# One rotary product for two heads' queries, with the swapped halves moved into the stored key

## The chip, the cores and the metric

The kernel runs on all 8 cores of one Trainium2 chip. Cores 0 to 3 are one die, 4 to 7 the other. Each core works on its own 1024 of the 8192 tokens and the cores do not exchange data. The metric is the device time of the slowest core, in microseconds. A run is "fast" when neither die's granted TensorE clock fell below the other's and its time is within 1.5% of the fastest; in "slow" runs one die runs at a granted clock of 0.81 to 0.98 and the time is up to 18% longer.

## The reference

The operation is a decoder block: a gated convolution and latent attention in parallel, then a gated feed-forward. The part that matters is the query and the key of the attention. There are 16 heads; a query has 128 plain and 64 rotary dimensions, and the 64 rotary dimensions of the key are the same for all heads.

```python
q = (rmsnorm(q_lat, q_a_g) @ w_q_b).reshape(b, s, 16, 192)
# ... k_nope, v from the latent; k_rope shared by all heads
q = apply_rope_tail(rmsnorm(q, q_norm_g), cos, sin)
k = apply_rope_tail(rmsnorm(k, k_norm_g), cos, sin)
y_mla = causal_block_attention(q, k, v) @ w_mla_out

def apply_rope_tail(x, cos, sin):          # on the last 64 of 192
    x1, x2 = split(x_r, 2)                 # 32 and 32
    rot = concat([x1 * cos - x2 * sin, x2 * cos + x1 * sin])
```

## The kernel before

Data lie with features on the 128 partitions (rows) and tokens on the free dimension (columns). One head's query is made in three tiles of 348, 348 and 344 tokens. The rotation needs `x2` where `x1` is, so the weights of each head hold its rotary columns twice, the second time with the halves exchanged; the product gives both copies in one 128-row result, of which only 64 rows are new information.

```python
def QN(t):                                   # plain part, 6 matmuls
    for k in range(6):
        mm(PS[p][:, 0:n], w[:, k, 0:128], qn[:, k, off:off + n], ...)
    act(sqn[:, 0:n], PS[p][:, 0:n], AF.Square, ...)
    act(qraw[:, 0:n], PS[p][:, 0:n], AF.Copy, ...)

def QR(t):                                   # rotary part, 6 matmuls, rows 64..127 are the swapped copy
    for k in range(6):
        mm(PS[p][:, 0:n], w[:, k, 128:256], qn[:, k, off:off + n], ...)
    act(sqr[0:64, 0:n], PS[p][0:64, 0:n], AF.Square, ...)
    tt(qt1[0:64, 0:n], PS[p][0:64, 0:n], CSq[0:64, off:off + n], ALU.mult, ...)
    tt(qt2[0:64, 0:n], PS[p][64:128, 0:n], CSq[64:128, off:off + n], ALU.mult, ...)
    tt(qr_[0:64, 0:n], qt1[0:64, 0:n], qt2[0:64, 0:n], ALU.add, ...)

def QS(t):                                   # sum of squares over rows: 2 matmuls against ones
    mm(PS[p][:, 0:n], ones, sqn[:, 0:n], True, False, ...)
    mm(PS[p][:, 0:n], ones, sqr[:, 0:n], False, True, ...)     # rows 64..127 are zeros
    rsq(rsqh[:, 0:n], PS[p][:, 0:n], 192.0, ...)
    stt(Qn[hb][...], qraw, gqe, rsqh, ALU.mult, ALU.mult, ...)
    tt(Qr[hb][0:64, ...], qr_[0:64], rsqh[0:64], ALU.mult, ...)
```

The score of a block of 128 keys takes two matmuls per query stretch: one with the plain key, one with the rotary key `krope`, whose rows 64 to 127 are zeros (so are those of `Qr`).

The order of instructions is decided when the program is built. Streams of small units (score steps, probability-times-value steps, key, value, query and convolution units) are merged by a list scheduler in the kernel: it keeps an estimate of when each engine is free and takes next the unit that TensorE would wait least for, and among equals the one with the lowest target position `pos`.

```python
t = S.ready(PE, u.need() if callable(u.need) else u.need, u.room) if u.pe else 0.0
...
key = (int(max(0.0, t - S.free[PE]) / 0.1), u.pos)
if best is None or key < best[0]:
    best = (key, s, b)
...
weight = [(912 - A_(kb // 4)) / 960.0 + 0.45 for kb in range(32)]     # where a score step belongs in its head
for us, span in ((kq, 0.85), (vq, 0.95), (qq, 0.85)):                 # next head's units, spread over this head
    for i, u in enumerate(us):
        u.pos = h - 1 + span * i / len(us)
...
rate = (sum(u.pe for u in st_c.units) - 22.0) / (NH + 0.3)            # convolution units per head
```

The constants 0.45, 0.85 and 22.0 are set by hand.

## Time and profile before

| | |
|---|---|
| time, median of 4 fast runs | 2668.1 us |
| attention stage (from the first 390-column matmul to the last attention matmul) | 992.6 us |
| stage before / after it, core 1 | 207.9 / 1465.3 us |

The cores view of before gives each core's span and mean granted clock. This profile fell into a slow run; cores 4 to 7 are left aside.

```profile
core 1: 2665.7 us, clock 0.996
...
core 3: 2662.7 us, clock 0.997
...
core 6: 2922.4 us, clock 0.898
...
die 0 (median of its cores): 2665.0 us, clock 0.997
die 1 (median of its cores): 2914.3 us, clock 0.892
```

The busy line of the page of core 1 (time, share of the span and number of instructions for each engine; PEld is the weight load, which overlaps) and the chain that ended last:

```profile
PE 2578.4 (97%) x18530; PEld 1637.9 (61%) x18530; DVE 1530.1 (57%) x3086; ACT 983.6 (37%) x1716; POOL 192.4 (7%) x330
...
PE 89%; DVE 3%; DMA 3%; issue 2%; ACT 2%; SPq 0%; DVEq 0%; ACTq 0%; POOL 0%; POOLq 0%
```

TensorE is busy 97% of the span, and the chain is 89% TensorE: it is the bound. The stage of interest is attention. The windows view of core 1 over this stage (stretch, its length, then busy time of TensorE, weight loads, VectorE, ScalarE and POOL, the clock, and the DMA share and rate):

```profile
207.00:1201.00 994.00, 969.44 (x7943) 608.13 (x7944) 732.20 (x1825) 688.06 (x1268) 32.72 (x62) 1.00 0.20 39
```

VectorE and ScalarE are busy 74% and 69% of the stage, TensorE 98%. The lines named in the profile are those of helpers: L509 issues the matmuls, L516 the ScalarE operations, L527, L523 and L540 VectorE's operations on two tensors, on two tensors and a scalar, and its copies. (All are one higher after the change.) What TensorE waits for in the stage, from the waits view of core 1 (total us, times, longest):

```profile
PE ps L509 <- ACT arena L516: 9.6, 26, 0.9
PE ps L509 <- DVE arena L527: 7.7, 19, 1.1
PE ps L509 <- DVE arena L523: 3.8, 6, 1.2
PE ps L509 <- DVE arena L540: 0.4, 2, 0.2
```

These are waits of up to 1.2 us, 21.5 us in all, none of which stands out. The matmuls, VectorE and ScalarE operations of the query work, from the groups by shape of core 1 (count, busy us, mean ns of one):

```profile
L509 PE MATMUL ps<-arena 128*128 128x348 bf16 x448 | 81.4, 311 | 2.0 <-ACT arena L516 1.7
...
L509 PE MATMUL ps<-arena 128*128 128x344 bf16 x224 | 40.3, 309 | 0.0
...
L527 DVE TENSOR_TENSOR arena<-ps,arena 64x348 f32<-64x348 f32 x64 | 33.1, 517 | 18.2 <-ACT arena L516 15.3 <-PE ps L509 2.0
...
L527 DVE TENSOR_TENSOR arena<-arena 64x348 f32<-64x348 f32 x32 | 16.2, 508 | 0.9 <-DVE arena L527 0.2
L527 DVE TENSOR_TENSOR arena<-arena 64x348 bf16<-64x348 f32 x32 | 16.2, 506 | 0.0
...
L516 ACT ACTIVATE arena<-ps 64x348 bf16<-64x348 f32 x32 | 14.4, 451 | 16.9 <-PE ps L509 16.8
```

672 matmuls of 348 or 344 columns are the query work. Their mean of 311 ns is not what one costs: matmuls overlap, and their ends are modelled. What one costs is the time from its start to the next one's start, in a run of equal ones: 147 ns for 348 columns.

"Columns" is what the stage's matmuls would take back to back, (columns / 2.4 GHz + 2.5 ns, at least 25 ns) each; this fits the median start to start of every shape that appears in runs within 1.2 ns. "Waits" is the rest: the time from start to start above that. (The waits view shows less: it counts a gap only from the modelled end of a matmul, which for 348 columns lies 311 ns after its start, not 147.)

### The profile page before, as it was taken

The page shows a single profiled execution, that of the slowest core. Times are in us where ns is not written, and L with a number is a line of the kernel's source. Part 1 is how long each engine was busy: PE and PEld are TensorE (multiplying, and loading weights), DVE is VectorE, ACT ScalarE, POOL GpSimd, SP SyncE. Part 2 cuts the span into 40 slices and gives each one's busy share as a digit, 9 for nine tenths or more (in the row PEclk, how much of TensorE's full clock was granted, in tenths as well). Part 3 has the DMA queues.
Part 4 walks back from the last instruction along what each step waited for, and adds up shares of the span by engine and source line. Part 5 has one row for each costly group of instructions (what it writes and reads, how often), then busy time and mean ns, then how long its engine had stood idle before and what let it go on. Part 6 is the DMA issues. An engine that isn't in the chain of part 4 may idle for free.

```text
span 2922.4 us, 51158 instructions; the slowest of 8 cores (2662.7 to 2922.4 us)
## 1 busy us (share of the span) xinstructions
PE 2841.3 (97%) x18415; PEld 1726.9 (59%) x18530; DVE 1534.9 (53%) x3086; ACT 983.2 (34%) x1716; POOL 191.8 (7%) x330
## 2 busy tenths in 40 slices
PE   4999999999999999999999999999999999999999
PEld 2886565656666665666666665554466456645653
DVE  3973777777877777411111112664266436634652
ACT  4864777776777777211101132000000000000000
POOL 1010000000000000000000000000000000000000
PEclk9999999999999999999888888888888888888888
DMA  9663111111202113444334733333433343344346
GB/s 198 153 112 59 22 32 30 36 29 25 44 22 39 20 34 100 80 74 71 59 61 66 173 64 59 64 60 56 73 59 63 56 70 65 54 62 72 59 68 148
DMA packets 65685, 196.68 MB, mean 67 GB/s; under 512 B 7328, under 2 KB 8608, under 8 KB 64416
## 3 DMA queue, kind: packets, MB, share of 16 engines
q0 software_dynamic: 46800, 145.91, 30.8%
q1 hardware_dynamic: 18640, 47.51, 5.0%
q8 instruction: 154, 2.52, 0.3%
q14 instruction: 91, 0.75, 0.1%
HBM read 323.44 MB, written 15.83 MB: 116 GB/s over the span
## 4 chain that ended last, share of the span: by engine, by line
PE 89%; DVE 4%; issue 3%; ACT 2%; DMA 2%; SPq 0%; DVEq 0%; ACTq 0%; POOL 0%; POOLq 0%
PE ps L509 89%; DVE arena L527 2%; ACT arena L516 2%; DVE arena L523 2%; DMA arena<-wkvin 1%; DMA arena<-xg 0%; SPq L543 0%; DVE arena L540 0%; DVEq L196 0%; ACTq L196 0%; DVE arena L533 0%; POOL arena L543 0%; POOLq L196 0%; SPq L196 0%
## 5 line engine op out<-in xcount | busy, mean ns | idle before, releaser
L509 PE MATMUL ps<-arena 128*128 128x390 bf16 (+11 forms) x18415 | 2841.3, 319 | 77.7 <-ACT arena L516 31.8
L509 PEld LDWEIGHTS ps<-arena 128*128 128x128 bf16 x18530 | 1726.9, 102 | 1191.5 <-issue 368.0
L527 DVE TENSOR_TENSOR arena<-ps,arena 128x390 f32<-128x390 f32 (+6 forms) x744 | 378.2, 511 | 1079.4 <-PE ps L509 979.6
L527 DVE TENSOR_TENSOR arena<-arena 128x130 bf16<-128x130 bf16 (+18 forms) x1522 | 669.7, 479 | 249.1 <-ACT arena L516 223.2
L516 ACT ACTIVATE arena<-arena 128x256 f32<-128x256 f32 (+13 forms) x412 | 267.5, 674 | 1114.7 <-DVE arena L523 966.9
L516 ACT ACTIVATE arena<-ps,arena 128x128 bf16<-128x128 f32 (+10 forms) x672 | 440.7, 672 | 499.1 <-PE ps L509 464.3
L523 DVE SCALAR_TENSOR_TENSOR arena<-arena 128x1024 f32<-128x1024 f32 (+9 forms) x499 | 371.9, 762 | 31.6 <-ACT arena L516 5.8
L516 ACT ACTIVATE arena<-ps 128x512 bf16<-128x512 f32 (+13 forms) x627 | 312.8, 515 | 204.8 <-PE ps L509 198.9
L543 POOL DMA_DIRECT2D arena<-wall x294 | 171.5, 584 | 2563.2 <-PE ps L509 2511.7
L536 DVE TENSOR_SCALAR arena<-arena 128x1024 f32<-128x1024 f32 (+1 forms) x90 | 72.3, 804 | 0.0
L523 DVE SCALAR_TENSOR_TENSOR arena<-ps,arena 128x256 bf16<-128x256 f32 (+1 forms) x80 | 33.2, 465 | 12.0 <-PE ps L509 6.9
L540 DVE COPY arena<-ps 128x456 f32<-128x456 f32 (+2 forms) x64 | 27.2, 425 | 2.1 <-PE ps L509 1.1
L543 POOL DMA_DIRECT2D arena<-xg x30 | 16.0, 549 | 141.5 <-PE ps L509 50.6
L533 DVE TENSOR_SCALAR arena<-arena 128x390 f32<-128x390 f32 (+2 forms) x29 | 16.2, 560 | 2.0 <-DVE arena L540 0.2
L516 ACT ACT_TABLE_LOAD x5 | 6.4, 1283 | 30.0 <-DVE arena L523 17.2
L527 DVE TENSOR_TENSOR arena<-arena,ps 128x390 bf16<-128x390 f32 (+1 forms) x24 | 12.3, 511 | 1.3 <-PE ps L509 0.7
L540 DVE CAST arena<-arena 128x1028 f32<-128x1028 int32 (+1 forms) x5 | 3.6, 719 | 4.7 <-DMA arena<-posg 4.3
L540 DVE COPY arena<-arena 128x6 f32<-128x6 f32 (+1 forms) x24 | 3.8, 158 | 1.0
L961 POOL MEMSET arena<- 128x4096 bf16 x1 | 3.6, 3560 | 0.0
L1145 DVE MEMSET arena<- 64x1040 bf16 x2 | 1.9, 925 | 0.4 <-issue 0.4
L767 DVE MEMSET arena<- 128x128 bf16 x1 | 0.2, 165 | 1.2 <-PEq L420 1.2
L543 POOL DMA_DIRECT2D arena<-cst x1 | 0.7, 720 | 0.0
(6 smaller groups left out, 1.2 us busy)
## 6 DMA issues: line engine op xcount, KB each, us to landing
arena<-wall POOLq DMA_DIRECT2D x182, 512.0 KB, 5.3
arena<-wall POOLq DMA_DIRECT2D x64, 352.0 KB, 4.5
arena<-xg POOLq DMA_DIRECT2D x22, 512.0 KB, 9.8
arena<-xo SPq DMA_DIRECT2D x16, 520.0 KB, 20.3
arena<-xg SPq DMA_DIRECT2D x8, 1024.0 KB, 6.3
arena<-wall POOLq DMA_DIRECT2D x32, 256.0 KB, 4.0
outT<-arena SPq DMA_DIRECT2D x32, 256.0 KB, 3.8
arena<-wall POOLq DMA_DIRECT2D x16, 384.0 KB, 4.7
```

Of the source, the lines that this page charges most:

```text
L509: S.add(PE, lambda e: e.matmul(out, lhsT=lhsT, rhs=rhs, start=start, stop=stop), reads, writes, cost=max(width(rhs) / 2400.0, 0.055) + 0.003)
L516: S.add(ACT, lambda e: e.activation(out=out, in_=in_, func=func, **kw), reads, writes, cost=c)
L523: S.add(DVE, lambda e: e.scalar_tensor_tensor(out=out, in0=in0, scalar=scalar, in1=in1, op0=op0, op1=op1), reads, writes, cost=dcost(out, ...
L527: S.add(DVE, lambda e: e.tensor_tensor(out=out, in0=in0, in1=in1, op=op), reads, writes, cost=dcost(out, in0, in1) + held)
L533: S.add(DVE, lambda e: e.tensor_scalar(out=out, in0=in0, scalar1=s1, scalar2=None, op0=op0), reads, writes, cost=c)
L536: S.add(DVE, lambda e: e.tensor_scalar(out=out, in0=in0, scalar1=s1, scalar2=s2, op0=op0, op1=op1), reads, writes, cost=c)
L540: S.add(DVE, lambda e: e.tensor_copy(out=out, in_=in_), reads, writes, cost=dcost(out, in_))
L543: S.add(eng, lambda e: e.dma_start(out=out, in_=in_), reads=reads, writes=writes, chan=chan, cost=in_.shape[0] * width(in_) * esz(in_.dtyp ...
L767: S.add(DVE, lambda e: e.memset(ones, 1.0), writes=[Tones], cost=0.2)
L961: f_h.units.append(Unit(lambda: S.add(POOL, lambda e: e.memset(krope, 0.0), writes=Tkr, cost=3.5), 0.0, pos=-8.0, ok=lambda: not f_w.units ...
L1145: S.add(DVE, lambda e, i_=i_: e.memset(Qr[i_][64:128, :], 0.0), writes=[TQr[i_]])
```

## The change

A score is a sum over rows, so the swap can be done on either side of it. The change stores the key's rotary rows a second time, halves exchanged, in the rows of `krope` that held zeros; the query needs `x * cos` in its first 64 rows and `x * (sin, -sin)` in the others, from the same unswapped `x`. The 64 rows of weight columns that this frees take the next head's rotary columns: one product per pair of heads. The rotary squares are added into the plain ones, so that one matmul against ones is enough.

```diff
 def weight_plan():
-        plan.append((("hq", h), "wq", 0, 6, 256 * h, 256))
+        if h % 2 == 0:
+            plan.append((("hq", h // 2), "wq", 0, 6, 192 * h, 384))
...
-    f_h.units.append(Unit(lambda: S.add(POOL, lambda e: e.memset(krope, 0.0), ...
+    def krot():
+        for r, q in ((64, 32), (96, 0)):
+            dma(SP, krope[r:r + 32, :], krope[q:q + 32, :], "krs%d" % q, reads=Tkr, writes=Tkr)
...
+    def QR(t):                       # in every second head only
+        for k in range(6):
+            mm(PS[p][:, 0:n], w[:, k, 256:384], qn[:, k, off:off + n], k == 0, k == 5, ...)
+        act(sqr[:, t, 0:n], PS[p][:, 0:n], AF.Square, ...)
+        for x, y in ((0, 3), (1, t)):
+            r = slice(64 * x, 64 * x + 64)
+            for o in (slice(0, 64), slice(64, 128)):
+                tt(qrot[o, y, 0:n], PS[p][r, 0:n], CSq[o, off:off + n], ALU.mult, ...)
     def QN(t):
...
+        tt(sqn[r, 0:n], sqn[r, 0:n], sqr[r, t, 0:n], ALU.add, ...)
     def QS(t):
-        mm(PS[p][:, 0:n], ones, sqn[:, 0:n], True, False, ...)
-        mm(PS[p][:, 0:n], ones, sqr[:, 0:n], False, True, ...)
+        mm(PS[p][:, 0:n], ones, sqn[:, 0:n], True, True, ...)
-        tt(Qr[hb][0:64, ...], qr_[0:64, 0:n], rsqh[0:64, 0:n], ALU.mult, ...)
+        tt(Qr[hb][:, ...], qrot[:, y, 0:n], rsqh[:, 0:n], ALU.mult, ...)
...
-    gst, Tgst = P4.slabs(2, [NA], BF16, "gst")      # staging of the convolution's result
+    gst, Tgst = P4.tile([NA], BF16, "gst")
-    rate = (sum(u.pe for u in st_c.units) - 22.0) / (NH + 0.3)
+    LAST, ODD = 22.0, 2.6                           # 2.6 us more convolution in every second head
...
-        if kb == 0 and not (free_(4) and free_(5)):
+        if kb == 0 and not (free_(4) and free_(5) and F.at("fin") >= 2 * h - 1):
```

The last line is needed: without it, this order puts a head's first probability-times-value step ahead of the read of the finished bank.

More of the change, by code (lines that the diff above doesn't have):

```diff
@@ L361 @@
 for _n, _w in [("g1", 16), ("bgate", 32), ("convw", 24), ("qag", 6), ("kvag", 4), ("gqn", 1), ("gkn", 1),
-               ("gq2", 1), ("gk2", 1), ("sg2", 1), ("g2", 16), ("fcw", 264), ("fcb", 88),
+               ("gq2", 1), ("gk2", 1), ("sg2", 1), ("sq2", 1), ("g2", 16), ("fcw", 264), ("fcb", 88),
                ("invf", 1), ("invflo", 1), ("mask", 528)]:
@@ L812, in gains @@
         tt(gks, C("gk2"), C("sg2"), ALU.mult, [Tcst], [Tgks])
-        tt(gqs, C("gq2"), C("sg2"), ALU.mult, [Tcst], [Tgqs])
+        tt(gqs, C("gq2"), C("sq2"), ALU.mult, [Tcst], [Tgqs])
     def own_table():
@@ L960, in build_program @@
     f_t.units.append(Unit(lambda: S.add(DVE, lambda e: e.memset(sqkr[64:128, :, :], 0.0), writes=Tsqkr), 0.0, pos=-8.5))
-    f_h.units.append(Unit(lambda: S.add(POOL, lambda e: e.memset(krope, 0.0), writes=Tkr, cost=3.5), 0.0,
-                          pos=-8.0, ok=lambda: not f_w.units and not f_w.pend))
     f_h.units.append(Unit(lambda: lpost(0, 4), 0.0, pos=-8.0,
@@ L1083, in qnorm @@
         F.mark("qn", 0)
+    def krot():
+        for r, q in ((64, 32), (96, 0)):
+            dma(SP, krope[r:r + 32, :], krope[q:q + 32, :], "krs%d" % q, reads=Tkr, writes=Tkr)
     for n in range(18):
+        if n == 4:
+            st_l.units.append(Unit(krot, 0.0, pos=-9.0))
         i, t = divmod(n, 3)
@@ L1110, in build_program @@
         TQr.append(t)
-    ring("B", [P4.take(3072), P4.take(2048), P4.take(3072), P4.take(2048)], [3072, 2048] * 2,
-         [b for b, pl in enumerate(plan) if pl[0][0] in ("hq", "hkv")])
+    for name, kind, k, nbytes in (("Q", "hq", 1, 4608), ("B", "hkv", 2, 2048)):
+        ring(name, [P4.take(nbytes) for _ in range(k)], [nbytes] * k,
+             [b for b, pl in enumerate(plan) if pl[0][0] == kind])
     zvs, Tzvs = P4.tile([390], F32, "zvs")
@@ L1116, in build_program @@
     ycs, Tycs = P4.tile([390], F32, "yc")
-    gst, Tgst = P4.slabs(2, [NA], BF16, "gst")
+    gst, Tgst = P4.tile([NA], BF16, "gst")
     sqk, Tsqk = P4.slabs(2, [512], BF16, "sqk")
     sqn, Tsqn = P4.tile([348], BF16, "sqn")
-    sqr, Tsqr = P4.tile([348], BF16, "sqr")
+    sqr, Tsqr = P4.slabs(3, [348], BF16, "sqr")
     rsqh, Trsqh = P4.tile([348], F32, "rsqh")
     qraw, Tqraw = P4.tile([348], F32, "qraw")
-    qt1, Tqt1 = P4.tile([348], F32, "qt1")
-    qt2, Tqt2 = P4.tile([348], F32, "qt2")
-    qr_, Tqr_ = P4.tile([348], F32, "qr")
+    qrot, Tqrot = P4.slabs(4, [348], F32, "qrot")
     ast, Tast = P4.slabs(2, [NA], BF16, "ast")
@@ L1143, in build_program @@
     Tgd = [T("gd%d" % i) for i in range(8)]
-    for i_ in range(2):
-        S.add(DVE, lambda e, i_=i_: e.memset(Qr[i_][64:128, :], 0.0), writes=[TQr[i_]])
-    S.add(DVE, lambda e: e.memset(sqr[64:128, :], 0.0), writes=[Tsqr])
     def fbank():
@@ L1201, in mulb @@
                         def mulb():
-                            tt(gst[:, i % 2, off:off + n], ycs[:, 0:n], PS[p][:, 0:n], ALU.mult, [Tycs, TP[p]],
-                               [Tgst[i % 2]])
+                            tt(gst[:, off:off + n], ycs[:, 0:n], PS[p][:, 0:n], ALU.mult, [Tycs, TP[p]],
+                               [Tgst])
                             if t == 1:
-                                dma(SP, gcv_d[i * 128:(i + 1) * 128, :], gst[:, i % 2, :], "gd%d" % (i % 2),
-                                    reads=[Tgst[i % 2]], writes=[Tgd[i]])
+                                dma(SP, gcv_d[i * 128:(i + 1) * 128, :], gst, "gd",
+                                    reads=[Tgst], writes=[Tgd[i]])
                         mulb()
@@ L1219, in start @@
             if not st:
-                st["wq"], st["Twq"] = wget(("hq", h))
                 st["wkv"], st["Twkv"] = wget(("hkv", h))
@@ L1257, in VU @@
             act(dst, src, AF.Copy, [TP[p]], [TVh[hb][g]])
-        def QN(t):
-            start()
-            w, Tw = st["wq"], st["Twq"]
+        def QR(t):
+            w, Tw = wget(("hq", h // 2))
             off, n = QT[t]
@@ L1264, in QN @@
             for k in range(6):
-                mm(PS[p][:, 0:n], w[:, k, 0:128], qn[:, k, off:off + n], k == 0, k == 5, [Tw, Tqn[k]], [TP[p]])
+                mm(PS[p][:, 0:n], w[:, k, 256:384], qn[:, k, off:off + n], k == 0, k == 5, [Tw, Tqn[k]], [TP[p]])
+            act(sqr[:, t, 0:n], PS[p][:, 0:n], AF.Square, [TP[p]], [Tsqr[t]])
+            for x, y in ((0, 3), (1, t)):
+                r = slice(64 * x, 64 * x + 64)
+                for o in (slice(0, 64), slice(64, 128)):
+                    tt(qrot[o, y, 0:n], PS[p][r, 0:n], CSq[o, off:off + n], ALU.mult, [TP[p], TCSq], [Tqrot[y]],
+                       0.09 * (o != r))
+        def QN(t):
+            w, Tw = wget(("hq", h // 2))
+            off, n = QT[t]
+            p = fbank()
+            x = h % 2
+            for k in range(6):
+                mm(PS[p][:, 0:n], w[:, k, 128 * x:128 * x + 128], qn[:, k, off:off + n], k == 0, k == 5, [Tw, Tqn[k]],
+                   [TP[p]])
             act(sqn[:, 0:n], PS[p][:, 0:n], AF.Square, [TP[p]], [Tsqn])
             act(qraw[:, 0:n], PS[p][:, 0:n], AF.Copy, [TP[p]], [Tqraw])
-        def QR(t):
-            start()
-            w, Tw = st["wq"], st["Twq"]
-            off, n = QT[t]
-            p = fbank()
-            for k in range(6):
-                mm(PS[p][:, 0:n], w[:, k, 128:256], qn[:, k, off:off + n], k == 0, k == 5, [Tw, Tqn[k]], [TP[p]])
-            act(sqr[0:64, 0:n], PS[p][0:64, 0:n], AF.Square, [TP[p]], [Tsqr])
-            tt(qt1[0:64, 0:n], PS[p][0:64, 0:n], CSq[0:64, off:off + n], ALU.mult, [TP[p], TCSq], [Tqt1])
-            tt(qt2[0:64, 0:n], PS[p][64:128, 0:n], CSq[64:128, off:off + n], ALU.mult, [TP[p], TCSq], [Tqt2], 0.09)
-            tt(qr_[0:64, 0:n], qt1[0:64, 0:n], qt2[0:64, 0:n], ALU.add, [Tqt1, Tqt2], [Tqr_])
+            r = slice(64 * x, 64 * x + 64)
+            tt(sqn[r, 0:n], sqn[r, 0:n], sqr[r, t, 0:n], ALU.add, [Tsqn, Tsqr[t]], [Tsqn])
         def QS(t):
@@ L1283, in QS @@
             p = fbank()
-            mm(PS[p][:, 0:n], ones, sqn[:, 0:n], True, False, [Tones, Tsqn], [TP[p]])
-            mm(PS[p][:, 0:n], ones, sqr[:, 0:n], False, True, [Tones, Tsqr], [TP[p]])
+            y = t if h % 2 else 3
+            mm(PS[p][:, 0:n], ones, sqn[:, 0:n], True, True, [Tones, Tsqn], [TP[p]])
             rsq(rsqh[:, 0:n], PS[p][:, 0:n], 192.0, [TP[p]], [Trsqh])
@@ L1289, in QS @@
                 [Tqraw, Tgqe, Trsqh], [TQn[hb]])
-            tt(Qr[hb][0:64, off:off + n], qr_[0:64, 0:n], rsqh[0:64, 0:n], ALU.mult, [Tqr_, Trsqh], [TQr[hb]])
+            tt(Qr[hb][:, off:off + n], qrot[:, y, 0:n], rsqh[:, 0:n], ALU.mult, [Tqrot[y], Trsqh], [TQr[hb]])
         def end(which):
@@ L1295, in end @@
                 wdone(("hkv", h))
-            if left["q"] == 0 and which == "q":
-                wdone(("hq", h))
-        left = {"k": 12, "v": 8, "q": 9}
+            if left["q"] == 0 and which == "q" and h % 2:
+                wdone(("hq", h // 2))
+        left = {"k": 12, "v": 8, "q": 6 if h % 2 else 9}
         def U(which, f, *a):
@@ L1316, in prologue_units @@
         for t in range(3):
-            qq += [Unit(U("q", QN, t), 0.87, ok=okq, bank=True), Unit(U("q", QR, t), 0.87, bank=True),
-                   Unit(U("q", QS, t), 0.3, need=[Tsqn, Tsqr], strict=True, bank=True)]
+            qq += [Unit(U("q", QR, t), 0.87, ok=okq, bank=True)] * (h % 2 == 0)
+            qq += [Unit(U("q", QN, t), 0.87, ok=okq, bank=True),
+                   Unit(U("q", QS, t), 0.15, need=[Tsqn], strict=True, bank=True)]
         for us, span in ((kq, 0.85), (vq, 0.95), (qq, 0.85)):
@@ L1455, in build_program @@
     kdone = lambda h: st_k.done >= 12 * (h + 1) and (st_k.done > 12 * (h + 1) or not st_k.pend)
-    qdone = lambda h: st_q.done >= 9 * (h + 1) and (st_q.done > 9 * (h + 1) or not st_q.pend)
+    qend = lambda h: 15 * (h // 2) + (15 if h % 2 else 9)
+    qdone = lambda h: st_q.done >= qend(h) and (st_q.done > qend(h) or not st_q.pend)
     vdone = lambda n: st_v.done > n or (st_v.done == n and not st_v.pend)
@@ L1465, in build_program @@
     st_c.units = conv_units()
-    rate = (sum(u.pe for u in st_c.units) - 22.0) / (NH + 0.3)
-    c = 0.0
+    LAST, ODD = 22.0, 2.6
+    extra = [0.0 if h % 2 else ODD for h in range(NH - 1)] + [LAST]
+    rate = (sum(u.pe for u in st_c.units) - sum(extra)) / (NH + 0.3)
+    spans = [(-0.3, 0.3, 0.3 * rate)] + [(h, 1.0, rate + extra[h]) for h in range(NH)]
+    c, n = 0.0, 0
     for u in st_c.units:
-        u.pos = c / rate - 0.3 if c < rate * (NH - 0.7) else NH - 1 + (c - rate * (NH - 0.7)) / (rate + 22.0)
+        while c >= spans[n][2] and n < NH:
+            c -= spans[n][2]
+            n += 1
+        u.pos = spans[n][0] + spans[n][1] * c / spans[n][2]
         c += u.pe
@@ L1698, in prepare_inputs @@
     wkvin = np.ascontiguousarray(wkvin.reshape(16, 128, 640).transpose(1, 0, 2)).reshape(128, 16 * 640)
-    wq = np.empty((768, NH * 256), f32)
-    for h in range(NH):
-        b0 = h * 192
-        wq[:, 256 * h:256 * h + 192] = wq0[:, b0:b0 + 192]
-        wq[:, 256 * h + 192:256 * h + 224] = wq0[:, b0 + 160:b0 + 192]
-        wq[:, 256 * h + 224:256 * h + 256] = wq0[:, b0 + 128:b0 + 160]
+    wq = wq0.reshape(768, NH // 2, 2, 192)
+    wq = np.concatenate([wq[:, :, :, 0:128].reshape(768, NH // 2, 256), wq[:, :, :, 128:192].reshape(768, NH // 2, 128)],
+                        axis=2).reshape(768, NH * 192)
     mats = {"w_in": w_in0, "wq": wq, "w_kvb": np.asarray(w_kv_b, f32)[0], "w_co": np.asarray(w_conv_out, f32)[0],
@@ L1729, in prepare_inputs @@
     put("gkn", gk[0:128, None])
-    put("gq2", np.concatenate([gq[128:192], gq[160:192], gq[128:160]])[:, None])
+    put("gq2", np.concatenate([gq[128:192], gq[128:192]])[:, None])
     put("gk2", np.concatenate([gk[128:192], gk[160:192], gk[128:160]])[:, None])
     put("sg2", np.concatenate([np.ones(64, f32), -np.ones(32, f32), np.ones(32, f32)])[:, None])
+    put("sq2", np.concatenate([np.ones(96, f32), -np.ones(32, f32)])[:, None])
     put("g2", _chunked(np.asarray(ln2_g, f32)[0], 16))
```

## The prediction

> **What bounds the kernel now.** I read the undisturbed die: cores 0 to 3 span 2663 to 2667 us at a granted clock of 0.996 to 0.997; cores 4 to 7 took 2908 to 2922 us at 0.89 (cores view). On core 0 the matmul engine is busy 2572 us of 2667 (96%), and the chain of waits is 85% PE. In the windows view, attention (480 to 1180 us) shows PE busy 679 of 700 us, VectorE 537, ScalarE 504: PE bounds it, with 20 us of waits in 420 to 1240 us (waits view), half for ScalarE, half for VectorE.
>
> **What is removed.** The instruction order has 18530 matmuls before, 18338 after. The 192 that go are 348 or 344 columns wide: 6 x 3 x 8 from one rotary product for two heads, 3 x 16 from the second statistics matmul. Start to start in runs of equal matmuls on core 0, 348 columns take 147 ns and 344 take 146. The Trainium skill states this ("TensorE: Matmul & The Clock Gate", section "Wait — 56ns, not 53.3ns?": N / 2.4 GHz + about 2.5 ns when warm), and this trace agrees. 128 x 147 + 64 x 146 ns = 28.2 us, all inside attention.
>
> **What is added or moved.**
> - ScalarE: 24 squares fewer at 0.45 us: 11 us less.
> - VectorE, per pair of heads and query tile: before six 64-row operations (0.51 us each, 3.1 us); after four such and two bf16 additions into the squares, which I estimate at 0.34 us, between 0.22 us for 130 columns and 0.42 us for 512 in bf16. Sum 2.7 us, so about 10 us less in all. The final multiply covers 128 rows for 64 at the same 0.50 us.
> - The statistics matmul now waits for ScalarE's square, then VectorE's addition: some 0.5 us more latency, filled by other matmuls.
> - Two 256 KB copies within SBUF during the query latents, some 50 us before their first use; a 3.6 us POOL memset and three VectorE memsets go. None is on the path.
> - The score product has as many matmuls as before.
> - The pair's query weights have one slot; in the new order 20 us of PE work lie between its last use and the next, against about 5 us for a load.
>
> **How much counts.** PE is the bound and its stream is in order, so nearly all of the 28.2 us should come off. Less filler and longer statistics latency leave VectorE and ScalarE at a higher share of a shorter stage, and the order crams one head's query work (head 14) together. I take off 2 us: a saving of 26 us.
>
> **Predicted time: 2642 us, 8 in 10 between 2633 and 2652.** Chances: faster by over 2% 0.01, within 2% 0.98, slower by over 2% 0.01.
>
> **What would show it right.** On a fast core: 192 fewer matmuls; PE busy time down 26 to 30 us; the time from first to last attention matmul 23 to 30 us shorter, the stages before (215 us) and after (about 1450 us) unchanged within 2 us; VectorE busy down 5 to 15 us, ScalarE 8 to 14 us; PE's waits in attention still 15 to 30 us in sum; the copies absent from the chain.
>
> **What would make it wrong.** PE's waits for VectorE growing by over 10 us, because the 64-row operations cross partition halves (output rows 64 to 127 from rows 0 to 63) and hold the queue, or at head boundaries, where a new condition may delay the first probability-times-value step; a late weight load into the single slot; a lower granted clock now that the zero rows carry data.

## More of the kernel before

Before, the stage has 7937 matmuls, 940.3 us of columns and 52.3 us of waits.

On two cores of each profile about 80 matmul records are missing, so their split is left aside.

## The result and the profile after

The changed kernel took 2645.7 us (median of 4 fast runs, 2641.9 to 2648.0) against 2668.1 us (2665.8 to 2669.0): 22.4 us less, inside the predicted range, 3.7 us above its centre. The ratio is 0.9916, 95% interval 0.9899 to 0.9933. Ratios in this text are the mean time of one kernel's fast runs over that of the other's fast runs of the same rounds, so not quite the ratio of the medians.

The lines of after that answer to those of before follow. The cores view of after; this profile is of a fast run:

```profile
core 1: 2638.7 us, clock 0.996
core 2: 2631.5 us, clock 0.997
...
core 4: 2646.2 us, clock 0.996
...
die 0 (median of its cores): 2636.8 us, clock 0.997
die 1 (median of its cores): 2638.7 us, clock 0.997
```

The busy line and the chain of core 1, from the page of after:

```profile
PE 2551.7 (97%) x18338; PEld 1621.5 (61%) x18338; DVE 1525.0 (58%) x3083; ACT 969.3 (37%) x1692; POOL 184.2 (7%) x321
...
PE 82%; DVE 7%; DMA 4%; issue 4%; ACT 2%; SPq 0%; DVEq 0%; ACTq 0%; POOL 0%; POOLq 0%
```

The windows view of after over its attention stage on core 1, with the same columns:

```profile
206.00:1176.00 970.00, 941.80 (x7751) 591.27 (x7752) 726.49 (x1822) 674.02 (x1243) 28.50 (x54) 1.00 0.20 39
```

What TensorE waits for in this stage, core 1 of after:

```profile
PE ps L510 <- DVE arena L528: 9.8, 21, 1.4
PE ps L510 <- ACT arena L517: 8.2, 24, 0.8
PE ps L510 <- DVE arena L524: 3.8, 3, 1.5
PE ps L510 <- DVE arena L541: 3.6, 4, 1.2
```

The groups by shape of core 1 of after, TensorE, VectorE and ScalarE:

```profile
L510 PE MATMUL ps<-arena 128*128 128x348 bf16 x320 | 59.6, 311 | 0.3
...
L510 PE MATMUL ps<-arena 128*128 128x344 bf16 x160 | 29.8, 309 | 0.8 <-DVE arena L528 0.7
...
L528 DVE TENSOR_TENSOR arena<-ps,arena 64x348 f32<-64x348 f32 x64 | 33.1, 518 | 8.4 <-ACT arena L517 5.9
...
L524 DVE SCALAR_TENSOR_TENSOR arena<-arena 128x348 bf16<-128x348 f32 x32 | 18.5, 579 | 8.2 <-ACT arena L517 8.1
...
L528 DVE TENSOR_TENSOR arena<-arena 128x348 bf16<-128x348 f32 x32 | 16.4, 514 | 0.0
...
L528 DVE TENSOR_TENSOR arena<-arena 64x348 bf16<-64x348 bf16 x32 | 10.7, 334 | 8.3 <-ACT arena L517 7.9
...
L517 ACT ACTIVATE arena<-ps 128x348 bf16<-128x348 f32 x48 | 22.1, 459 | 12.3 <-PE ps L510 12.3
```

Two lines above are both written 128x348 bf16 on VectorE: the scalar_tensor_tensor of the plain part, which was there before, and the tensor_tensor that took the place of the 64-row one. 192 matmuls are gone, and TensorE's busy time fell by 26.7 us (2578.4 to 2551.7). The attention stage fell from 992.6 to 969.4 us (median of the cores), that is by 23.2 us. Columns fell by exactly the 28.2 us that were to go, 940.3 to 912.1. The other 5.0 us are in the waits: 52.3 before, 57.3 after. In the waits view it is 21.5 to 25.4 us on core 1, inside the 15 to 30 us that the prediction named. One line is new in size: the waits for L541, VectorE's copies, here of a finished bank, 0.4 us before (there L540) and 3.6 us after.

### The profile page after: what moved, and what is told of

It reads as the page before. It is cut to its first block, busy times and chain, and to the rows that moved or that the text cites. A ratio compares the mean times of both kernels' runs of the same rounds, so it can differ in the third digit from the quotient of the medians.

```text
span 2646.2 us, 50879 instructions; the slowest of 8 cores (2631.5 to 2646.2 us)
## 1 busy us (share of the span) xinstructions
PE 2551.6 (96%) x18338; PEld 1621.0 (61%) x18338; DVE 1525.0 (58%) x3083; ACT 968.7 (37%) x1692; POOL 184.7 (7%) x321
## 4 chain that ended last, share of the span: by engine, by line
PE 83%; DVE 6%; DMA 4%; issue 4%; ACT 3%; SPq 0%; DVEq 0%; ACTq 0%; POOL 0%; POOLq 0%
PE ps L510 83%; DVE arena L528 4%; ACT arena L517 3%; DVE arena L524 2%; DMA outT<-arena 2%; DMA arena<-wkvin 1%; DMA arena<-xg 1%; DMA arena<-wall 0%; SPq L544 0%; DVE arena L541 0%; DVEq L196 0%; DVE arena L534 0%; ACTq L196 0%; DVE arena L537 0%; POOL arena L544 0%
## 5 line engine op out<-in xcount | busy, mean ns | idle before, releaser
L510 PE MATMUL ps<-arena 128*128 128x390 bf16 (+11 forms) x18338 | 2551.6, 300 | 81.2 <-ACT arena L517 43.7
L510 PEld LDWEIGHTS ps<-arena 128*128 128x128 bf16 x18338 | 1621.0, 98 | 1011.3 <-issue 168.5
L528 DVE TENSOR_TENSOR arena<-ps,arena 128x390 f32<-128x390 f32 (+7 forms) x744 | 374.0, 510 | 813.6 <-PE ps L510 720.1
L528 DVE TENSOR_TENSOR arena<-arena 128x130 bf16<-128x130 bf16 (+19 forms) x1522 | 665.4, 474 | 243.0 <-ACT arena L517 214.6
L517 ACT ACTIVATE arena<-arena 128x256 f32<-128x256 f32 (+14 forms) x412 | 267.5, 675 | 909.7 <-DVE arena L524 791.4
L517 ACT ACTIVATE arena<-ps,arena 128x910 bf16<-128x910 f32 (+10 forms) x672 | 437.7, 673 | 444.9 <-PE ps L510 405.6
L517 ACT ACTIVATE arena<-ps 128x512 bf16<-128x512 f32 (+9 forms) x603 | 299.7, 519 | 200.7 <-PE ps L510 189.9
L541 DVE COPY arena<-ps 128x456 f32<-128x456 f32 (+2 forms) x64 | 27.1, 424 | 2.1 <-PE ps L510 1.3
L517 ACT ACT_TABLE_LOAD x5 | 6.4, 1283 | 28.2 <-DVE arena L524 14.2
L528 DVE TENSOR_TENSOR arena<-arena,ps 128x390 bf16<-128x390 f32 (+1 forms) x24 | 12.3, 511 | 3.2 <-DMA gcv_d<-arena 2.5
L541 DVE CAST arena<-arena 128x1028 f32<-128x1028 int32 (+1 forms) x5 | 3.5, 697 | 3.6 <-DMA arena<-posg 3.2
L541 DVE COPY arena<-arena 128x6 f32<-128x6 f32 (+1 forms) x24 | 3.8, 159 | 1.1
## 6 DMA issues: line engine op xcount, KB each, us to landing
arena<-xo SPq DMA_DIRECT2D x16, 520.0 KB, 23.6
```

The lines of the kernel that those rows point to most:

```text
L510: S.add(PE, lambda e: e.matmul(out, lhsT=lhsT, rhs=rhs, start=start, stop=stop), reads, writes, cost=max(width(rhs) / 2400.0, 0.055) + 0.003)
L517: S.add(ACT, lambda e: e.activation(out=out, in_=in_, func=func, **kw), reads, writes, cost=c)
L528: S.add(DVE, lambda e: e.tensor_tensor(out=out, in0=in0, in1=in1, op=op), reads, writes, cost=dcost(out, in0, in1) + held)
L541: S.add(DVE, lambda e: e.tensor_copy(out=out, in_=in_), reads, writes, cost=dcost(out, in_))
```

## The experiments

The theory after this first reading ("columns"): TensorE's columns set the time, and each matmul taken away is worth its 147 ns. The open question is what raised the waits by 5 us, out of 28. Four suspects: the new addition on VectorE and the longer way to the statistics matmul; the head boundary, where the copy is waited for; the single staging buffer of the convolution; the new share of convolution per head. A fifth came up only later: the order itself. All times of the attention stage are medians over the cores of one profile (of the die that was not slowed, where one was); they vary by under 3 us between the cores of one run.

### Control

No edit: the kernel before, once more.

> The kernel before, unchanged, run once more for a profile in the fast state on all eight cores and for the noise. Both theories: within 0.3% of before. Attention, from the first 390-column matmul to the last attention matmul, 992.5 us on every core as on the four undisturbed cores of the first profile. If the spread between cores that the changed kernel showed (2631 to 2646 us) is the output tail and not the change, it shows here too, at 8 us or more between the fastest and the slowest core; if it comes of the change, the cores here lie within 5 us.

The ratio was 0.9994 (0.9975 to 1.0014), attention 992.6 us again. The profile fell into a slow run once more, so the spread is read from the fast runs' spans: in the three of this run the fastest and the slowest core lie 9.7 to 14.0 us apart (2650.7 to 2660.4; 2653.9 to 2664.7; 2652.1 to 2666.1). Over the 24 fast runs of before whose cores are listed it is 6.1 to 14.9 us, in the four of after 10.5 to 15.1. The spread is therefore not of the change. Most of it arises behind attention: the stage itself is the same on all cores within 0.2 us before and 1.7 us after, while the stage behind it runs from 1457.3 to 1467.6 us over the eight cores of after (and the stage ahead of it from 204.5 to 208.8 us).

### Each half of the change by itself: stat2, dupqr, onestat

dupqr, from the changed kernel: the shared product is computed twice.

```diff
-            for k in range(6):
+            for k in [0, 1, 2, 3, 4, 5] * 2:
                 mm(PS[p][:, 0:n], w[:, k, 256:384], ...)
```

> The changed kernel with every shared rotary product computed twice into the same bank (144 matmuls more, same result). Theory PE: attention longer by 144 x 147 ns = 21.1 us less what the extra matmuls cover of waits, so 17 to 22 us, and the time near 2665 us. Rival (waits for VectorE and ScalarE set the stage, the matmuls only fill them): less than 12 us longer.

Attention took 991.3 us, 21.9 us longer than after (columns +21.2, waits +0.7); the ratio to before was 0.9994. The merged product is worth its matmuls in full, a little over the expected 21.1.

stat2, from the changed kernel: the second statistics matmul comes back, over the 64 rows of the head, and the addition goes.

```diff
-            tt(sqn[r, 0:n], sqn[r, 0:n], sqr[r, t, 0:n], ALU.add, ...)
-            mm(PS[p][:, 0:n], ones, sqn[:, 0:n], True, True, ...)
+            mm(PS[p][:, 0:n], ones, sqn[:, 0:n], True, False, ...)
+            mm(PS[p][:, 0:n], ones[r], sqr[r, t, 0:n], False, True, ...)
```

> The changed kernel with the second statistics matmul put back (48 matmuls, contracting over the 64 rows of its head) and the VectorE addition into the squares taken out. Theory PE (matmul columns set the time): attention 5 to 8 us longer than in the changed kernel (969 us), 48 x 147 ns = 7.1 us. Rival (the longer way through ScalarE and VectorE to the statistics matmul is what ate part of the gain): attention no longer than in the changed kernel, or shorter, as the waits that it caused go away.

Attention took 983.5 us, 14.1 longer: twice what either theory allowed for. The trace shows why, and it is a fault of the experiment. These are the starts around one of the 48 matmuls on core 0, in ns from its own start (shape as rows x columns of the moving data):

```
128x512 -459   128x348 -243   64x348 0   128x348 +251   128x348 +409   128x348 +556
```

A 64-row matmul (the trace lists it as 64*128, the others as 128*128) starts 243 ns (median of core 1) after a 348-column one and the next starts 250 ns later, where 147 would do: about 200 ns more than its columns for each of the 48, 9.6 us in all. The Trainium skill has this ("TensorEngine Tiling (Array Packing)", section "Key Properties": "Changing tiling mode (not just tile) drains the TensorE"), and these times agree with it, though a drain as such is not seen in the trace. The run tells nothing of the addition.

onestat, from the kernel before: only the addition and the single statistics matmul (cut: the unit of QS is also told of its new cost and need, as in the change).

```diff
+            tt(sqn[0:64, 0:n], sqn[0:64, 0:n], sqr[0:64, 0:n], ALU.add, ...)
-            mm(PS[p][:, 0:n], ones, sqn[:, 0:n], True, False, ...)
-            mm(PS[p][:, 0:n], ones, sqr[:, 0:n], False, True, ...)
+            mm(PS[p][:, 0:n], ones, sqn[:, 0:n], True, True, ...)
```

> The kernel before with only the one statistics matmul per tile taken over (VectorE adds the 64 rotary rows' squares into the others; 48 matmuls fewer, 48 VectorE additions more, no change to the rotary product, its table, the key or the buffers). Theory PE: attention 5 to 8 us shorter than before (992.5 us), time near 2661 us. Rival (the addition's latency eats it): under 3 us shorter.

Attention took 995.2 us, 2.6 longer than before, with 7.1 us of columns fewer: waits of 61.9 us. The ratio was 1.0015 (0.9991 to 1.0039, from two fast runs). Both expected numbers were missed on the side of the rival. Taken alone it says that the addition eats all of its gain and more; the next two runs test just that in the changed kernel, and the section on the order comes back to onestat.

### The addition by itself: noadd, stat2b

noadd, from the changed kernel (wrong):

```diff
-            tt(sqn[r, 0:n], sqn[r, 0:n], sqr[r, t, 0:n], ALU.add, ...)
```

> The changed kernel without VectorE's addition of the rotary squares (wrong result on purpose: the heads' scale misses the rotary part); every matmul stays. So far the merged rotary product was worth its 144 matmuls in full (attention 21.9 us longer when they were put back), and the single statistics matmul alone was worth nothing (attention 2.6 us longer than before, not 7 shorter). Theory addition (the addition and the wait for it on VectorE eat what the 48 matmuls save): attention 4 to 7 us shorter than the changed kernel's 969.4 us. Rival (the shortfall is the luck of another order, with its waits at head boundaries): within 1.5 us of 969.4.

Attention took 969.5 us against 969.4. The theory that the addition costs the 5 us falls, as far as one order can tell: all 48 of them, 16.0 us of VectorE time with the latency behind it, cost the stage nothing here. (Each of these edits also lays the order out anew, and an order by itself moves the stage by some us, as shown below.) (The output still passed the comparison with the reference, although the heads' scale is wrong; that comparison would not have caught this mistake.)

stat2b, from the changed kernel: the second statistics matmul over all 128 rows, with ones in one head's rows and zeros in the other's, and no addition.

```diff
+    hones, Thones = P0.tile([2, 128], BF16, "hones")          # per head: ones in its 64 rows
-            tt(sqn[r, 0:n], sqn[r, 0:n], sqr[r, t, 0:n], ALU.add, ...)
-            mm(PS[p][:, 0:n], ones, sqn[:, 0:n], True, True, ...)
+            mm(PS[p][:, 0:n], ones, sqn[:, 0:n], True, False, ...)
+            mm(PS[p][:, 0:n], hones[:, x, :], sqr[:, t, 0:n], False, True, ...)
```

> The changed kernel with the second statistics matmul put back over all 128 rows (its stationary matrix has ones in the rows of the one head, zeros in the other's) and without the addition: what the run with 64-row matmuls was meant to be, but there each of these 48 took some 200 ns more than its columns. Theory addition: 7.1 us of matmuls more, 4 to 7 us of waits fewer, attention 969 to 973 us. Rival (matmul columns count, the addition is free): 975 to 978 us. If the row count was what made the first run long, this one is well under its 983.5 us.

Attention took 976.9 us, 7.5 longer, for 7.1 us of columns: inside the rival's range. So in the changed kernel both halves measured as worth their columns in full, 144 matmuls 21.9 us and 48 matmuls 7.5 us. Put back together they would give 998.8 us, while the kernel before, which has the same matmuls, takes 992.6. The missing 5 to 6 us do not show in either half. And 983.5 less 976.9, the 6.6 us between 64 and 128 rows, is what the stage lost to the 64-row matmuls; that it is less than the 9.6 us counted at them means 3 us fewer waits elsewhere, which were not followed up.

### The new waits one by one: room, cpfirst, gst2, odd0

room tells the scheduler that a head's first probability-times-value step needs the two banks that the last head's result is copied out of. cpfirst puts that copy ahead of an addition on VectorE. gst2 gives the part of the convolution's staging tile that is written first a second buffer. odd0 spreads the convolution evenly.

```diff
# room
         st_p.units.append(Unit(lambda si=si: step_p(si), c / 3, need=[TPT[si % NPT]],
+                               room=[TP[4], TP[5]] if kb == 0 else [],
# cpfirst
-        stt(accb, acc[:, 0, lo:hi], 1e-30, acc[:, 1, lo:hi], ALU.add, ALU.add, Tacc, [Taccb])
         cp(pvr, PS[4 + half][:, 0:HALF], [TP[4 + half]], [Tpvr])
+        stt(accb, acc[:, 0, lo:hi], 1e-30, acc[:, 1, lo:hi], ALU.add, ALU.add, Tacc, [Taccb])
# gst2 (cut)
-    gst, Tgst = P4.tile([NA], BF16, "gst")
+    gst, Tgst = P4.tile([780], BF16, "gst")
+    gs2, Tgs2 = P4.slabs(2, [260], BF16, "gs2")
# odd0
-    LAST, ODD = 22.0, 2.6
+    LAST, ODD = 22.0, 0.0
```

> The changed kernel, where the order of matmuls is told that the first probability-times-value step of a head needs the banks that the last head's result is being copied out of (so that it puts other matmuls first). Theory boundary (4 us of the 28 were lost at head boundaries, where this step now waits for VectorE's copy): the wait of 456-column matmuls for the copy falls from 3.9 us to under 1 us, attention 2 to 4 us shorter than the changed kernel's 969 us. Rival (the wait moves elsewhere, as VectorE and ScalarE are late in any case): the copy wait falls, attention within 1 us.

> The changed kernel with the copy out of the finished bank put ahead of the 0.63 us addition of the two partial sums on VectorE. Theory boundary: the copy wait shrinks from 3.9 us by about 0.6 us at each of 7 boundaries, to about 1 us or less; attention 2 to 4 us shorter. Rival: the wait moves to the denominator matmul, which now waits longer for that addition, attention within 1 us.

> The changed kernel with a second buffer for the part of the convolution's result that is written first, so that VectorE doesn't wait for the store of the last group. Theory boundary: VectorE's 2.5 us of waits for that store vanish and the two 260-column waits of PE (1.4 us) with them; attention 0.5 to 2 us shorter. Rival: no change within 0.5 us, as PE has other work then.

> The changed kernel with the convolution spread evenly over the heads, as before, not with 2.6 us more in every second one. Theory boundary: even heads are left with less filler than odd ones, attention 1 to 6 us longer. Rival (the order's choice of filler hardly matters): within 1 us.

Attention took 968.5, 969.2, 969.0 and 970.8 us, against 969.4 (ratios to before 0.9923, 0.9929, 0.9920, 0.9933; after had 0.9916). The first three stay short of what the boundary theory expected of them and inside the rival's range; odd0 is inside its range at the low end, 1.4 us longer, and says only that the even share is no better. In cpfirst the waits for the copy fell only from 3.6 to 2.5 us on core 1, while those for L528 rose from 9.8 to 11.2; in gst2 VectorE's wait of 1.8 us for the store was gone and TensorE's waits stayed as they were. room is the one to look at. What TensorE waits for in its attention stage, core 1:

```profile
PE ps L510 <- ACT arena L517: 9.7, 32, 0.7
PE ps L510 <- DVE arena L528: 8.6, 25, 1.1
PE ps L510 <- DVE arena L524: 3.8, 3, 1.5
PE ps L510 <- DMA arena<-wall: 0.8, 1, 0.8
```

The line of L541 is gone, 3.6 us of it, as planned; but the waits for ScalarE (L517) went from 8.2 to 9.7 us, and by the full sum from the starts the waits of the stage were 56.4 us against 57.3. In every kernel derived from the change so far they lie between 56.4 and 58.7 us, whatever named wait was taken away or matmul put back (64-row matmuls aside). A wait that is taken away comes back elsewhere in the order.

### The order: neutral, best

Since none of the parts of the change that were tried brings the waits, the last suspect is what they are all laid out by. The scheduler's own estimate of the attention stage can be printed when the program is built. It is no time of the chip; but its differences agree with the measured ones within 1.7 us, save for stat2, whose 64-row matmuls it costs like the others:

| kernel | scheduler's estimate, us, against before | attention measured, us | against before | columns | waits |
|---|---|---|---|---|---|
| before | 1003.6 | 992.6 | | 940.3 | 52.3 |
| onestat | +2.1 | 995.2 | +2.6 | 933.3 | 61.9 |
| dupqr | -2.8 | 991.3 | -1.3 | 933.3 | 58.0 |
| stat2 | -15.0 | 983.5 | -9.1 | 919.2 | 64.3 |
| stat2b | -15.0 | 976.9 | -15.7 | 919.2 | 57.7 |
| odd0 | -22.9 | 970.8 | -21.8 | 912.1 | 58.7 |
| after | -22.9 | 969.4 | -23.2 | 912.1 | 57.3 |
| gst2 | -22.9 | 969.0 | -23.6 | 912.1 | 56.9 |
| cpfirst | -25.1 | 969.2 | -23.4 | 912.1 | 57.1 |
| noadd | -23.4 | 969.5 | -23.1 | 912.1 | 57.4 |
| room | -25.0 | 968.5 | -24.1 | 912.1 | 56.4 |
| neutral | +8.2 | 1000.4 | +7.8 | 940.3 | 60.1 |
| best | -32.8 | 959.2 | -33.4 | 912.1 | 47.1 |

So I built 16 neighbours of before, each with one constant moved a little and the same instructions, and read their estimates: 1004.8 to 1012.8, mean 1008.9, none as low as the 1003.6 of before. 24 neighbours of after: 977.8 to 987.0, mean 982.5, around its 980.7. Mean to mean that is 26 us, close to the 28.2 us of columns.

These estimates the kernels give again (the table's came out within 0.2 us). 40 neighbours each, with 0.45, 0.85, 0.95 or 22.0 moved, gave 1003.6 to 1013.1 for before, mean 1008.8 against its own 1003.4, and 975.2 to 986.9 for after, mean 981.9. So before lies below all of its neighbours, and after near its mean. The same 40 moves price each half without the luck of one order: in the changed kernel, means of 1003.1 for dupqr, 988.6 for stat2b and 981.0 for noadd put the merged product at 21.2 us, the single statistics matmul at 6.6 and the addition at 1.0. But onestat's mean is 1007.0, only 1.8 below that of before for 7.1 us of columns. By the estimates, then, the order is not all of onestat's shortfall: about 5 us are lost there on average over these orders too. Why it is lost in the kernel before and not in the changed one was not tried.

Two runs put the order to the test. neutral is the kernel before with one constant moved:

```diff
-        for us, span in ((kq, 0.85), (vq, 0.95), (qq, 0.85)):
+        for us, span in ((kq, 0.85), (vq, 0.95), (qq, 0.87)):
```

> The kernel before with one constant of its build-time scheduler moved (the heads' query work is spread over 0.87 of the preceding head, not 0.85): the same instructions, in another order. Attention on the chip was 992.6 us before and 969.4 after; of it, columns 940.3 and 912.1, waits and gaps 52.2 and 56.7. Eight variants so far lay at 56 to 64 us of waits whatever was put back, so I now suspect that the order of before was a well-tuned one. The program's own scheduler estimates attention at 1003.6 us for before, 980.7 for the change, and 1004.8 to 1012.8 for sixteen builds of before with a constant moved a little; this one at 1011.8. Theory order: attention 997 to 1003 us, waits 57 to 62 us. Rival (something that the change brought causes the waits, not the order): attention within 1.5 us of 992.6.

best is the changed kernel with room, two constants picked by the lowest estimate of some 170 builds, and four output staging buffers:

```diff
+                               room=[TP[4], TP[5]] if kb == 0 else [],
-    weight = [(912 - A_(kb // 4)) / 960.0 + 0.45 for kb in range(32)]
+    weight = [(912 - A_(kb // 4)) / 960.0 + 0.65 for kb in range(32)]
-        for us, span in ((kq, 0.85), (vq, 0.95), (qq, 0.85)):
+        for us, span in ((kq, 0.85), (vq, 0.95), (qq, 0.84)):
-    ost, Tost = Pool_(A6, ARENA).slabs(2, [OWN], F32, "ost")
+    ost, Tost = Pool_(A6, ARENA).slabs(4, [OWN], F32, "ost")
```

> The changed kernel with its order tuned again and the output staged in four buffers instead of two. Order: the first probability-times-value step of a head is told of the banks that it needs, the weight of a step's fixed part is 0.65 instead of 0.45, the query work spreads over 0.84 instead of 0.85 (the scheduler's own estimate falls by 9.9 us). Theory order: attention 959 to 964 us instead of 969.4, waits 47 to 52 us. Rival (waits of 57 us are what the changed work costs in any order): attention 968 to 970. Output: PE's waits for VectorE's last additions, which themselves wait for the stores out, 2 to 9 us on the cores of the changed kernel, fall to under 2 us on all cores, and the slowest core lies less above the median core. Time 2629 to 2638 us against 2646 of the changed kernel.

The windows view of the attention stage of neutral, core 1:

```profile
205.00:1207.00 1002.00, 970.40 (x7945) 610.46 (x7946) 731.44 (x1825) 689.09 (x1268) 32.72 (x62) 1.00 0.20 39
```

The two largest waits of TensorE in that stage of neutral:

```profile
PE ps L509 <- ACT arena L516: 15.0, 31, 1.5
PE ps L509 <- DVE arena L527: 8.3, 23, 0.8
```

The windows view of the attention stage of best, core 1:

```profile
207.00:1168.00 961.00, 938.95 (x7754) 591.73 (x7755) 724.05 (x1822) 675.03 (x1245) 28.48 (x54) 1.00 0.20 39
```

And the two largest waits of TensorE in it:

```profile
PE ps L510 <- ACT arena L517: 8.9, 25, 0.8
PE ps L510 <- DVE arena L528: 4.9, 12, 0.7
```

neutral: the same instructions took 7.8 us longer in attention, and the whole kernel 1.0039 (1.0024 to 1.0054) of before, near 10 us. The waits went from 52.3 to 60.1 us, and TensorE waited 15.0 us for ScalarE instead of 9.6. best: 959.2 us in attention on every core within 0.4 us, waits of 47.1. Both are inside the range of the order theory and far outside the rival's. That best was picked does not tilt the comparison with before by the estimates: over 13 by 13 values of the two constants that best moves, no build of before came below its own 1003.4, while the changed kernel reached 974.5, and 969.5 with room.

best took 2637.5 us (median of its 4 fast runs, 2633.6 to 2642.0), ratio 0.9890 (0.9873 to 0.9906) to before, and is the fastest kernel here: about 8 us less than after by the medians. After did not run on the same chip in these rounds, so this difference is less certain than its cause in attention (10.2 us). The output half of best was a miss. VectorE's waits for the stores out in the last 100 us, in the waits view of core 4 of after:

```profile
DVE arena L528 <- DMA outT<-arena: 64.2, 15, 7.1
```

and of core 3 of best:

```profile
DVE arena L528 <- DMA outT<-arena: 67.7, 16, 7.7
```

Doubling the buffers did not shorten them (behind attention, over the eight cores, 56.2 to 66.5 us in after and 55.8 to 67.7 in best), and TensorE still waited 3.7 to 8.2 us for VectorE behind attention on four of the eight cores, where under 2 us was expected of all. Something behind the buffers is late on these cores: in the last 100 us the weights (352 KB each) and the stores (256 KB each) share the 16 DMA engines. What it is was not tried.

## Why the prediction was right

The range of 2633 to 2652 us would have held any saving from 16 to 35 us, so the hit alone says little; what follows is the mechanism.

- The bound and the size of the removal were right. Columns fell by 28.2 us in the trace, as summed from 147 and 146 ns. Putting the two parts back cost 21.9 and 7.5 us. The Trainium skill's figure of N / 2.4 GHz + 2.5 ns ("TensorE: Matmul & The Clock Gate", section "Wait — 56ns, not 53.3ns?") holds for them.
- The term that was mis-sized is "I take off 2 us". The waits took 5.0. The reason given, that VectorE and ScalarE stand at a higher share and the statistics take longer, is not what the runs bear out: taking the addition away changed nothing (noadd), and putting filler back didn't lower the waits (dupqr, 58.0). What the runs show is that the waits depend on the order: 8 us more with a constant moved in before, 10 us less with a new order of after. That before's order happened to be a good one among its neighbours (the estimates) and after's an ordinary one accounts for the 5 us; this last step is argued from the estimates and the two runs, not shown for every order. Mean to mean the estimates give 26 to 27 us, about the 26 that were predicted; that the chip gave 23.2 would then be the luck of before's order, which the prediction did not look at.
- The head boundary was named as a risk and did show 3.6 us of new waits, but room showed that they were not a loss of that size: taken away, they gave 0.9 us.
- VectorE's operations came out as costed: 506 to 518 ns for the 64-row and the 128-row ones, 334 ns for the bf16 addition (estimated at 0.34 us). The query's operations sum to 7.9 us less on VectorE (about 10 predicted) and 10.6 less on ScalarE (11 predicted). In all, VectorE's busy time fell by 5.1 us, at the edge of the 5 to 15 forecast; ScalarE's by 14.3, just over the 8 to 14 (the busy line counts overlapping operations once).
- The two copies landed by 218 us on core 1, 80 us ahead of the first attention matmul at 298, and are not in the chain. The clock stayed at 0.996 to 0.997 with data in the rows that held zeros. The weight slot cost no wait for the query weights; the one wait of TensorE for weights, up to 1.3 us and on five of the eight cores, was before a 260-column matmul, a convolution.
- One sign failed as it was worded. From the first to the last attention matmul the time fell by 36 us (913.9 to 877.7), not by 23 to 30: the new order puts 13 us of other work ahead of the first score. The stage has to be measured from where the mixed work begins.
- The prediction took the undisturbed die of a slow run (2663 to 2667 us) for the usual core. In fast runs the cores of before lie at 2650 to 2668, and the slowest of eight sets the time, before and after.

## What to carry to other kernels

Here TensorE was busy 97 to 98% of the stage, VectorE and ScalarE at most 75%. In the changed kernel, matmuls that were put back cost their columns (21.9 us for 21.2, 7.5 for 7.1), and this could be read from starts in the trace beforehand; in the kernel before, 48 matmuls taken away by themselves gained nothing (onestat). In a program whose order follows from constants, a change of the work lays the order out anew; here that was worth 5 us of 28, and twice as much was had back by choosing the order again (best). Judge such a change only with the order chosen equally well on both sides. Before a named wait is blamed, take it away alone: here the waits moved on and the stage stayed as long as it was.

## What the Trainium skill lacked or had wrong

- "Perfetto Trace Analysis", section "Optimization Strategy", advises finding what blocks the contended engine in its gaps and making that start sooner. It lacks the warning that in a fixed order the gap may only move: 3.6 us of waits for one copy taken away gave 0.9 us (room), and the same instructions in another order made 7.8 us (neutral).
- "TensorEngine Tiling (Array Packing)", section "Key Properties", says that a change of tiling mode drains TensorE, without a figure. Here a single 64-row matmul among 128-row ones cost about 200 ns more than its columns (243 and 250 ns from start to start instead of 147 each), and lengthened the stage by 6.6 us for 48 of them.
- "TensorE: Matmul & The Clock Gate", section "Seeing it yourself", says to budget 1.95 GHz, 13/16 of the clock, for sustained dense matmuls on all cores. Here all eight cores ran them for over 2600 us at a granted 0.995 to 0.999 in fast runs; only slow runs came down, to 0.81 to 0.98 on the slowed die, the lowest 0.814, which is about 13/16.
- No page says how far eight independent cores lie apart: 6.1 to 14.9 us from the fastest to the slowest in fast runs of before, 10.5 to 15.1 in those of after, most of it behind attention.
